# First modulation of four channel blocks: one-column products on TensorE in place of VectorE's chains of scaled additions

## The chip, the cores and the metric

The kernel runs on one core of a Trainium2 chip. A core has five engines that run their own instruction streams side by side: TensorE (PE in the profile; its weight loads are shown apart as PEld), VectorE (DVE), ScalarE (ACT), GpSimd (POOL) and SyncE (SP), which here issues the transfers. They wait for each other through semaphores. The metric is the device time of one execution in microseconds (us), the median of several runs.

## The reference, cut to what matters

The program is one layer of an encoder block on 1024 tokens with 1024 channels. Every sub-layer is wrapped in the same way:

```python
def sandwich(x, fn, g_pre, g_post, shift, scale, gate, res_w):
    h = rmsnorm(x, g_pre) * (1 + scale) + shift
    y = rmsnorm(fn(h), g_post)
    return x + res_w * gate * y

c_act = silu(c)                                   # c: one vector of 1024
mod = (c_act @ w_ada + b_ada).reshape(3, 3, 1024) # shift, scale, gate of each sub-layer
x = sandwich(x, swiglu_1, ..., mod[0, 0], mod[0, 1], mod[0, 2], 0.5)
x = sandwich(x, mixer,    ..., mod[1, 0], mod[1, 1], mod[1, 2], 1.0)
x = sandwich(x, swiglu_2, ..., mod[2, 0], mod[2, 1], mod[2, 2], 0.5)
```

The first sub-layer can't begin before its shift and scale exist: two vectors of 1024, each a product of `c_act` with a 1024 x 1024 piece of `w_ada` (4 MB apiece). `swiglu` then multiplies `h` with a gate and an up matrix of 1024 x 2816 each. All data is 32-bit float.

## The kernel before

Channels are held in 8 blocks of 128, one block on the 128 partitions; tokens in two halves of 512. A large product is made exact by splitting each operand into a high part of TensorE's reduced 32-bit format and the remainder: `hh` and `hl` for the modulated input, `wh` and `wl` for the weights. Three products (L433 to L435: hh with wh, hl with wh, hh with wl) then give one.

The change lies in `startup()`, which computes the first modulation block by block while it begins the first SwiGLU. All engines run this part in the written order (`manual_schedule` with all engines), so that an instruction that waits holds up everything behind it on its engine. For channel block j (0 to 7) the steps are:

- **Load** (L222): the 1024 x 128 pieces of `w_ada` for shift and scale, in four transfers into two tiles `rawa` (each holds 4 blocks of input channels, for both kinds).
- **Chain** (L231 to L235, VectorE): `acc` is the sum over the 8 blocks of input channels of `rawa` times the matching column of `c_act`, shift and scale side by side (128 x 256). This is done in two interleaved partial sums, two multiplications and six multiply-adds, and one addition joins them.
- **mv** (L240, TensorE): a product of `acc` with a column of ones sums over the partitions. The column (128 x 1) is what streams; `acc` is the stationary operand. There are two such products, shift and scale.
- **Set** (L245, L248, VectorE): bias and norm weight are added, which gives column j of `acol` (factor) and `scol` (shift).
- **h** (L321, L324 on ScalarE, L316 on VectorE): the transposed tokens `pt` (four transposes on TensorE, L1433) times factor plus shift, rounded into `hh`; once more unrounded into `h`; and `hl = h - hh`.
- **Parts** (`part(fb, sh, k)`): six products of 128 x 512 each, three for the gate and three for the up columns of weight block fb, with channel block k of the token half sh. Three weight blocks are begun in `startup`. Their split (`cut`, L136 on ScalarE for `wh`, L137 on GpSimd for `wl`) is queued in the same written order, so on ScalarE some splits come behind the h of a block.

In `startup` the order on TensorE is: transposes 0, mv 0, transposes 1, part(0,0,0), mv 1, transposes 2, part(0,0,1), part(1,0,0), mv 2, part(1,0,1), transposes 3, part(0,0,2), part(1,0,2), mv 3, the parts of weight block 2 with channel blocks 0 to 2, and then a loop over channel blocks 3 to 7 in which a block's chain on VectorE runs under eighteen products of the block before it. Behind the loop the second token half follows, and then sums of the halves of h on VectorE (L538, L544), which the next products need.

Of the kernel before, what the change touches and what calls it, by code (L numbers as in the profile page):

```python
# [21 lines left out]
DRAM = bass.MemoryType.DRAM  # L22
# [4 lines left out]
KB = D // P  # L27
# [13 lines left out]
SHARE = (3, 4, 4, 5, 5)  # L41
LEFT = 40.0
GATES = (2, 0, 2, 4)
NORM_ACT = ()
# [5 lines left out]
def kernel(  # L50
# [7 lines left out]
    nc = tc.nc  # L58
    x = x[0]
# [43 lines left out]
    def trbank(name):  # L103
        return ps[0].tile([P, 512], F32, tag="tr", bufs=2, name=nm(name))

# [1 line left out]
    colsA = cpool.tile([P, 104], F32, name="colsA")  # L107
# [25 lines left out]

# [1 line left out]
    def split(raw, hi, lo, eng=None):  # L135
# [19 lines left out]
    class Weights:  # L155
        """Splits the weights of a list in order, a few ahead of their use."""

# [14 lines left out]

# [1 line left out]
    c_act = cpool.tile([P, KB], F32, name="c_act")  # L174
# [62 lines left out]
    def ada_mv(acc):  # L237
# [3 lines left out]
        return pc  # L241

    def ada_set(j, pc):
        col = slice(j, j + 1)
        nc.vector.scalar_tensor_tensor(  # L245
            acol[0][:, col], pc[:, 1:2], colsA[:, 16 + j : 17 + j], colsA[:, 80 + j : 81 + j], op0=ALU.add, op1=ALU.mult
        )
        nc.vector.tensor_tensor(scol[0][:, col], pc[:, 0:1], colsA[:, 8 + j : 9 + j], op=ALU.add)  # L248
# [50 lines left out]

# [1 line left out]
    def rstd_of(src, eps):  # L301
# [36 lines left out]
    class Epilogue:  # L338
        """Residual update and next normalisation, in stages that lag the arithmetic by a token block each."""

# [50 lines left out]
        def finish(self, head, wait=HEAD_WAIT):  # L391
            """The last blocks, under the products of the next phase that need the first half only."""
            for i, _ in enumerate(head):
                if i >= wait or (self.ready and self.ready[0][0] == 0):
                    self.drain(1)
                if i == 0:
                    self.update(SB - 3)
                    self.update(SB - 2)
                    self.norm(SB - 3)
                if i == 2:  # L400
                    self.update(SB - 1)
                    self.norm(SB - 2)
                if i == 5:
                    self.norm(SB - 1)
            self.drain(KB)

        def push_last(self, sb, y, pd):
            """The last block: in halves, to end soon after the last product."""
            self.fetch(sb)
            xr = self.xr[sb]  # L410
            g = gtile[self.sub]
            sq = [small("sq"), small("sq")]
            halves = [slice(0, 512), slice(512, 1024)]
            for h, sl in enumerate(halves):
                junk = tmp[0].tile([P, D], BF16, tag="junk", bufs=2, name=nm("junk"))
                nc.vector.tensor_tensor(y[:, sl], y[:, sl], pd[h], op=ALU.add)
                nc.scalar.activation(junk[:, sl], y[:, sl], AF.Square, scale=D ** -0.5, accum_out=sq[h])
                if h == 0:
                    nc.vector.tensor_tensor(y[:, sl], y[:, sl], g[:, sl], op=ALU.mult)
            self.update(sb - 1)  # L420
            r = small("rstd")
            nc.vector.scalar_tensor_tensor(r, sq[0], self.eps, sq[1], op0=ALU.add, op1=ALU.add)
            nc.gpsimd.tensor_tensor(r, r, nhalf, op=ALU.pow)
            nc.vector.tensor_tensor(y[:, halves[1]], y[:, halves[1]], g[:, halves[1]], op=ALU.mult)
            for sl in halves:
                nc.vector.scalar_tensor_tensor(xr[:, sl], y[:, sl], r, xr[:, sl], op0=ALU.mult, op1=ALU.add)
                nc.sync.dma_start(self.xout[sb * P : (sb + 1) * P, sl], xr[:, sl])

# [1 line left out]
    def mm3(dst, w, kk, xhk, xlk, sh, first, last):  # L430
# [12 lines left out]

# [1 line left out]
    # The first column blocks of gate and up are plain products, while the halves of h are being summed. The others  # L445
    # take seven products of half blocks for eight (Strassen): with the gate [a b] and up [c e] rows of a block over
    # the halves of the channels, and h = [[w x] [y z]] over the halves of channels and tokens,
    #   1: (a+e)(w+z)  2: (c+e)w  3: a(x-z)  4: e(y-w)  5: (a+b)z  6: (c-a)(w+x)  7: (b-e)(y+z)
    #   gate = [1+4-5+7, 3+5], up = [2+4, 1-2+3+6]
    ORDER = (5, 1, 4, 6, 2, 3, 7)  # L450
    LAST_ORDER = (1, 6, 5, 4, 3, 2, 7)

    def ffn(sub, w_gu, w_down, hh, hl, xin, xout):
# [62 lines left out]

        # sums of the halves of h
        hs, dif = {}, {}
# [59 lines left out]

        # sums of the quarters of a weight block
        mixed = {}  # L580
# [81 lines left out]
        def up_phase(started):  # L662
            """All of act = silu(gate) * up, into DRAM."""
            for fb in range(started, direct):
# [5 lines left out]
            for fb in range(started, direct):  # L670
# [3 lines left out]
                finish(fb, 0)  # L674
            # what the first of the other blocks needs, in the order of its products
            def first_needs():
# [37 lines left out]

        # down projection, a few blocks of its contraction at a time
        chunks, fb0 = [], 0
# [4 lines left out]
        parts = {}  # L721

        def down_w(ci, n):
            """The n-th operand of a chunk: activations and weights of its blocks in turn."""
            if ci >= len(chunks) or n >= 2 * len(chunks[ci]):
                return
            fb, kind = chunks[ci][n // 2], n % 2
            raw = wpool.tile([P, 1024], F32, tag="raw", bufs=3, name=nm("rawd"))
            nc.sync.dma_start(raw, (act_d, w_down)[kind][fb * P : (fb + 1) * P, :])
            if kind == 0 and 0 < ci < len(chunks) - 1:  # L730
                hi, lo = (hpool.tile([P, 1024], F32R, tag="h", bufs=16, name=nm("ah")) for _ in range(2))
            elif kind == 1 and ci % 2 == 1:
                hi, lo = (wpool.tile([P, 1024], F32R, tag=t, bufs=4, name=nm("dh")) for t in ("wh", "wl"))
            else:
                hi, lo = t4("dh", F32R), t4("dl", F32R)
            split(raw, hi, lo, nc.gpsimd if kind else nc.vector)
            parts[ci, n] = hi, lo

        def down_phase(make, ahead):
# [4 lines left out]
            for sbs in (range(half), range(half, SB)):  # L744
                steps += [(ci, sb) for ci in (end - 1, end) for sb in sbs]
            # (updates, normalisations, transposed blocks of the first half) with each of the last steps
            last_steps = {
# [63 lines left out]

# [1 line left out]
    C_Q, C_K, C_V, C_XR, C_YR, C_GA, C_GR = 0, 512, 1024, 1536, 2560, 3584, 4608  # L813
# [197 lines left out]
    def att_phase(hh, hl, wts0, tg_dram, n_ga):  # L1011
        att_h, att_l = [], []
        with (
# [42 lines left out]

            # Projections as generators: one tensor-engine pass per step, cost in passes of 512.
            def pproj(w, sh):
# [74 lines left out]
            def vslice(p, h, kb):  # L1133
                # [token, block-in-tile 2, pair 2, (h0 hi, h0 lo, h1 lo, h1 hi) x 64]
                off = ((kb % 2) * 2 + p % 2) * 256 + h * P
                return vts[p // 2][kb // 2][:, off : off + P]
# [262 lines left out]

# [1 line left out]
    def startup(f1, hh, hl):  # L1401
# [40 lines left out]
        def chain(j, half):  # L1442
            ada_sum(raws[j], acc4[:, j % 2], ((0, 4, 1, 5), (2, 6, 3, 7))[half])

        def chain_seq(j, half):
            ada_sum(raws[j], acc4[:, j % 2], range(4 * half, 4 * half + 4))

        def mv(j):
            ada_set(j, ada_mv(acc4[:, j % 2]))

# [8 lines left out]
        trans(0, 0)  # L1459
        chain_seq(0, 0)  # L1460
        chain_seq(0, 1)
        f1.cut(0, 0)
        mv(0)
        trans(0, 1)
        h = h_act(0, 0)
        chain_seq(1, 0)
        h_lo(0, 0, h)
        chain_seq(1, 1)
        f1.cut(0, 1)
# [8 lines left out]
        f1.cut(1, 1)  # L1478
        chain(2, 0)
        chain(2, 1)  # L1480
        f1.part(1, 0, 0)
# [6 lines left out]
        f1.cut(2, 0)  # L1488
        chain(3, 0)
        chain(3, 1)  # L1490
        f1.cut(2, 1)
# [57 lines left out]

    # ==== program =========================================================  # L1550
    relrep = dpool.tile([HEADS, P * 767], F32, name="relrep")
# [83 lines left out]
```

## Time and profile before

| What | Value |
|---|---|
| Time, median of 3 runs | 2282.09 us (2281.98 to 2283.41) |
| Span of the profiled execution | 2280.4 us |
| TensorE busy in the span | 2212.2 us (97%) |
| VectorE, ScalarE, GpSimd busy | 1277.7, 925.0, 638.2 us |
| Mean granted TensorE clock | 0.991 of full speed |
| Transferred | 250.31 MB, mean 110 GB/s |

The profiled execution's own time is not listed apart from its span; the span runs from the first to the last instruction, and the median of the other runs is 1.7 us above it, which is what lies around it. TensorE is busy for 97% of the whole span, but that is a mean: in the first of forty slices (57 us each) it is 5 to 6 tenths busy, and in all the others 9 or more tenths. The first 50 us are the only stretch of that length in which TensorE waits for a large part.

### The profile page before, as it was taken

Reading aid. Unit: us, or ns where it says so; the run is one execution under the profiler, and the core shown is the slowest. Engines: PE = TensorE matmul, PEld = TensorE weight load, DVE = VectorE, ACT = ScalarE, POOL = GpSimd, SP = SyncE. Lnnn points to the kernel's source line nnn. Section 1 sums busy time; section 2 is a strip of 40 time slices with the busy share of each in tenths; the row PEclk is TensorE's granted clock in tenths of the full one; section 3 lists DMA queues with packets and bytes.
Section 4 is the critical chain, followed back from the end, with each engine's and each line's share of the span. In section 5 each row is a group of like instructions: output and inputs, shape, how many; then the busy total and the mean of one; then the engine's idle time right before and its main releaser. Section 6 shows DMA issues by size and latency. Waiting matters only on the chain.

```text
span 2280.4 us, 26502 instructions
## 1 busy us (share of the span) xinstructions
PE 2212.2 (97%) x10227; PEld 1837.4 (81%) x10227; DVE 1277.7 (56%) x1830; ACT 925.0 (41%) x1473; POOL 638.2 (28%) x449
## 2 busy tenths in 40 slices
PE   5989999999999999999999999999989999999998
PEld 3867888888788788888898988887878888888886
DVE  6675565545755677643336666546864444433444
ACT  3533333342223587821147777336433333342121
POOL 3433333322225311000021120006443333322324
PEclk9999999999999999999999999999999999999999
DMA  9322333345663211245312011554322222233223
GB/s 297 101 65 75 111 111 102 111 146 177 195 211 120 77 50 40 66 148 166 113 51 65 25 59 53 165 176 169 113 81 83 84 82 83 84 121 110 93 93 120
DMA packets 217749, 250.31 MB, mean 110 GB/s; under 512 B 10864, under 2 KB 172824, under 8 KB 217624
## 3 DMA queue, kind: packets, MB, share of 16 engines
q1 hardware_dynamic: 217512, 248.60, 34.7%
q8 instruction: 80, 1.31, 0.2%
q14 instruction: 45, 0.37, 0.0%
q10 hardware_dynamic: 112, 0.03, 0.0%
HBM read 203.51 MB, written 48.23 MB: 110 GB/s over the span
## 4 chain that ended last, share of the span: by engine, by line
PE 80%; DVE 8%; ACT 4%; issue 3%; DMA 2%; POOL 2%; SPq 1%; POOLq 0%; DVEq 0%; ACTq 0%
PE pd L766 19%; PE pj L433 6%; PE pj L434 6%; PE pj L435 6%; PE pj L1064 5%; PE psB L603 3%; PE psB L604 3%; PE psB L605 3%; PE psC L603 3%; PE psC L604 3%; PE psC L605 3%; PE psA L603 3%; PE psA L604 3%; PE psA L605 3%; PE pv L1111 1%
## 5 line engine op out<-in xcount | busy, mean ns | idle before, releaser
L766 PE MATMUL pd<-dh,ah 128*128 128x512 f32 x1440 | 346.9, 392 | 0.0
L766 PEld LDWEIGHTS pd<-dh,ah 128*128 128x128 f32 x1440 | 271.8, 189 | 57.0 <-POOL dh L137 0.5
L434 PE MATMUL pj<-hl,wh 128*128 128x512 f32 x576 | 226.9, 394 | 5.5 <-DVE hl L316 5.5
L779 DVE TENSOR_TENSOR yacc<-yacc,pd 128x512 f32<-128x512 f32 x190 | 121.9, 683 | 193.3 <-PE pd L766 193.2
L435 PE MATMUL pj<-hh,wl 128*128 128x512 f32 x576 | 227.1, 394 | 2.6 <-DVE wl L137 1.9
L433 PE MATMUL pj<-hh,wh 128*128 128x512 f32 x576 | 229.3, 398 | 0.0
L592 POOL TENSOR_TENSOR wsum<-raw,sr 128x512 f32<-128x512 f32 x70 | 101.0, 1443 | 318.4 <-DVE wm L596 313.8
L596 DVE TENSOR_TENSOR wm<-wsum,wm 128x512 fp32r<-128x512 f32 x185 | 146.8, 804 | 61.9 <-ACT wm L595 59.2
L595 ACT CAST wm<-wsum 128x512 fp32r<-128x512 f32 x185 | 112.5, 620 | 111.3 <-PE psB L605 83.9
L137 POOL TENSOR_TENSOR wl<-raw,wh 128x1024 fp32r<-128x1024 f32 x25 | 61.2, 2454 | 292.0 <-ACT wh L136 246.7
L136 ACT CAST wh<-raw 128x1024 fp32r<-128x1024 f32 (+1 forms) x86 | 86.8, 1011 | 129.2 <-PE pj L434 53.2
L434 PEld LDWEIGHTS pj<-hl,wh 128*128 128x128 f32 x576 | 109.4, 190 | 29.3 <-DVE hl L316 7.4
L435 PEld LDWEIGHTS pj<-hh,wl 128*128 128x128 f32 x576 | 109.3, 190 | 26.9 <-DVE wl L137 3.2
L603 PE MATMUL psB<-hh,wm 128*128 128x512 f32 x296 | 117.2, 396 | 14.1 <-DVE mixes L619 14.1
L433 PEld LDWEIGHTS pj<-hh,wh 128*128 128x128 f32 x576 | 109.5, 190 | 22.1 <-ACT hh L321 0.3
L137 DVE TENSOR_TENSOR wl<-raw,wh 128x1024 fp32r<-128x1024 f32 (+1 forms) x61 | 73.8, 1211 | 84.7 <-ACT wh L136 84.7
L604 PE MATMUL psB<-hl,wm 128*128 128x512 f32 x296 | 116.8, 395 | 0.0
L605 PE MATMUL psB<-hh,wm 128*128 128x512 f32 x296 | 116.8, 394 | 0.0
L603 PE MATMUL psC<-hh,wm 128*128 128x512 f32 x296 | 115.6, 391 | 0.5 <-ACT wm L595 0.5
L605 PE MATMUL psA<-hs,wm 128*128 128x512 f32 x296 | 115.3, 389 | 0.4 <-DVE wm L596 0.4
L605 PE MATMUL psC<-hh,wm 128*128 128x512 f32 x296 | 115.3, 390 | 0.0
L603 PE MATMUL psA<-hs,wm 128*128 128x512 f32 x296 | 115.3, 389 | 0.0
(296 smaller groups left out, 5218.0 us busy)
## 6 DMA issues: line engine op xcount, KB each, us to landing
rawa<-in_w_ada_dram SPq DMA_DIRECT2D x56, 512.0 KB, 3.7
raw<-in_ffn_w_gu_dram SPq DMA_DIRECT2D x49, 512.0 KB, 4.0
rawd<-act SPq DMA_DIRECT2D x44, 512.0 KB, 4.3
rawd<-in_ffn_w_down_dram SPq DMA_DIRECT2D x44, 512.0 KB, 4.1
raw<-in_w_in_dram SPq DMA_DIRECT2D x44, 512.0 KB, 3.8
sr<-in_ffn_w_gu_dram SPq DMA_DIRECT2D x39, 512.0 KB, 5.7
act<-act SPq DMA_DIRECT2D x37, 512.0 KB, 4.2
rawa<-in_w_ada_dram SPq DMA_DIRECT2D x32, 256.0 KB, 5.6
```

The costliest lines, as they stand in the source:

```text
L137: (eng or nc.vector).tensor_tensor(lo, raw, hi.bitcast(F32), op=ALU.subtract)
L433: nc.tensor.matmul(dst, wh[:, kk, :], xhk[:, sl], start=first, stop=False)
L434: nc.tensor.matmul(dst, wh[:, kk, :], xlk[:, sl], start=False, stop=False)
L435: nc.tensor.matmul(dst, wl[:, kk, :], xhk[:, sl], start=False, stop=last)
L595: nc.scalar.copy(t[:, 0], src)
L596: nc.vector.tensor_tensor(t[:, 1], src, t[:, 0].bitcast(F32), op=ALU.subtract)
L603: nc.tensor.matmul(dst, t[:, 0, kk, :], xh, start=first and kk == 0, stop=False, skip_group_check=True)
L604: nc.tensor.matmul(dst, t[:, 0, kk, :], xl, start=False, stop=False, skip_group_check=True)
L605: nc.tensor.matmul(dst, t[:, 1, kk, :], xh, start=False, stop=last and kk == 3, skip_group_check=True)
L766: nc.tensor.matmul(pd[h], a_[:, tk], w_[:, h * 512 : (h + 1) * 512], start=(i == 0 and j == 0), stop=(i == n - 1 and j == 2),)
L779: nc.vector.tensor_tensor(yacc[sb][:, sl], yacc[sb][:, sl], pd[h], op=ALU.add)
L1064: nc.tensor.matmul(d, a[:, k, :], b[k][:, sl], start=k == 0 and i == 0, stop=k == KB - 1 and i == 2)
```

## The change

For channel blocks 0 to 3 (`ON_PE = 4`) the chain on VectorE is left out. In its place `ada_direct` issues sixteen products on TensorE per block: for shift and for scale, eight products with the loaded `rawa` piece itself as stationary operand and one column of `c_act` as what streams, summed in the same column of PSUM. They stand at the place where the two products with the column of ones stood. Blocks 4 to 7 keep the chain. Nothing else moves in the written order; the lines of `startup` are shifted by the new function, and comments are dropped.

```diff
+ON_PE = 4
...
+    def ada_direct(raws):
+        pc = trbank("pcj")
+        for kind in range(2):
+            for k in range(KB):
+                nc.tensor.matmul(
+                    pc[:, kind : kind + 1], raws[k // 4][:, k % 4, kind, :], c_act[:, k : k + 1],
+                    start=k == 0, stop=k == KB - 1,
+                )
+        return pc
...
         def chain(j, half):
-            ada_sum(raws[j], acc4[:, j % 2], ((0, 4, 1, 5), (2, 6, 3, 7))[half])
-
-        def chain_seq(j, half):
-            ada_sum(raws[j], acc4[:, j % 2], range(4 * half, 4 * half + 4))
+            if j >= ON_PE:
+                ada_sum(raws[j], acc4[:, j % 2], ((0, 4, 1, 5), (2, 6, 3, 7))[half])
 
         def mv(j):
-            ada_set(j, ada_mv(acc4[:, j % 2]))
+            ada_set(j, ada_direct(raws[j]) if j < ON_PE else ada_mv(acc4[:, j % 2]))
...
         trans(0, 0)
-        chain_seq(0, 0)
-        chain_seq(0, 1)
         f1.cut(0, 0)
         mv(0)
         trans(0, 1)
         h = h_act(0, 0)
-        chain_seq(1, 0)
         h_lo(0, 0, h)
-        chain_seq(1, 1)
         f1.cut(0, 1)
         f1.part(0, 0, 0)
         mv(1)
...
-        chain(2, 0)
-        chain(2, 1)
         f1.part(1, 0, 0)
         mv(2)
...
-        chain(3, 0)
-        chain(3, 1)
         f1.cut(2, 1)
         f1.part(0, 0, 2)
         f1.part(1, 0, 2)
         mv(3)
```

On TensorE, before, from the last transposes of channel block 0 to the first product of the second column of block 0's part (`pcj` takes the modulation's two columns, `pj` the SwiGLU's sums):

```order
L1433 MATMUL pt_187<-ident,x_24_135 128x128
L240 MATMUL pcj_205<-ones_r,acc_17_117 128x1 x2
L1433 MATMUL pt_210<-ident,x_21_129 128x128
...
L433 MATMUL pj_232<-hh_100,wh_201 128x512
L434 MATMUL pj_232<-hl_108,wh_201 128x512
L435 MATMUL pj_232<-hh_100,wl_202 128x512
...
L435 MATMUL pj_236<-hh_100,wl_229 128x512
L240 MATMUL pcj_240<-ones_r,acc_17_117 128x1 x2
L1433 MATMUL pt_253<-ident,x_21_129 128x128
```

And the same stretch of TensorE now:

```order
L1444 MATMUL pt_187<-ident,x_24_135 128x128
L248 MATMUL pcj_196<-c_act,rawa_137 128x1 x4
L248 MATMUL pcj_196<-c_act,rawa_140 128x1 x4
L248 MATMUL pcj_196<-c_act,rawa_137 128x1 x4
L248 MATMUL pcj_196<-c_act,rawa_140 128x1 x4
L1444 MATMUL pt_215<-ident,x_21_129 128x128
...
L446 MATMUL pj_232<-hh_100,wl_225 128x512
L248 MATMUL pcj_236<-c_act,rawa_147 128x1 x4
L248 MATMUL pcj_236<-c_act,rawa_150 128x1 x4
L248 MATMUL pcj_236<-c_act,rawa_147 128x1 x4
L248 MATMUL pcj_236<-c_act,rawa_150 128x1 x4
L1444 MATMUL pt_263<-ident,x_21_129 128x128
```

Sixteen products stand where two stood, at the same place in the order: mv 1 is still behind the six products of block 0's part.

On VectorE, before, what stands between the setting of channel blocks 0 and 1:

```order
L245 SCALAR_TENSOR_TENSOR acol_81<-pcj_205,colsA 128x1 [waits PE_49]
L248 TENSOR_TENSOR scol_84<-pcj_205,colsA 128x1
L231 TENSOR_SCALAR acc_17_117<-rawa_147,c_act 128x256 [waits DMAHW6_49,DMAHW5_49]
L233 SCALAR_TENSOR_TENSOR acc_17_117<-rawa_147,c_act,acc_17_117 128x256 [waits DVE_49] x3
L316 TENSOR_TENSOR hl_108<-h_48_216,hh_100 128x512 [waits Activation_49]
L231 TENSOR_SCALAR acc_17_117<-rawa_150,c_act 128x256 [waits DMAHW7_49,DMAHW0_49]
L233 SCALAR_TENSOR_TENSOR acc_17_117<-rawa_150,c_act,acc_17_117 128x256 [waits DVE_49] x3
L235 TENSOR_TENSOR acc_17_117<-acc_17_117 128x256 [waits DVE_49]
L245 SCALAR_TENSOR_TENSOR acol_81<-pcj_240,colsA 128x1 [waits PE_49]
```

And now:

```order
L256 SCALAR_TENSOR_TENSOR acol_81<-pcj_196,colsA 128x1 [waits DVE_49,PE_49]
L259 TENSOR_TENSOR scol_84<-pcj_196,colsA 128x1
L327 TENSOR_TENSOR hl_108<-h_48_221,hh_100 128x512 [waits Activation_49]
L256 SCALAR_TENSOR_TENSOR acol_81<-pcj_236,colsA 128x1 [waits PE_49]
L259 TENSOR_TENSOR scol_84<-pcj_236,colsA 128x1
```

Nothing is left on VectorE there but the setting of the columns and the remainder `hl`. On SyncE the order of transfers is as before; the tiles that later loads reuse are now released by TensorE where VectorE released them.

## Rows read from the trace of the kernel before

**Rows 1.** Windows: time, each engine's busy us (instructions), granted clock, DMA share, GB/s.
```profile
13.40:48.40 35.00, 19.72 (x65) 13.99 (x66) 25.79 (x41) 10.18 (x12) 14.79 (x6) 0.97 1.17 294
48.40:53.30 4.90, 4.90 (x13) 3.84 (x14) 4.41 (x13) 1.45 (x2) 0.00 (x0) 0.50 1.07 381
53.30:93.30 40.00, 39.99 (x207) 33.17 (x206) 24.51 (x53) 24.72 (x36) 8.33 (x10) 1.00 0.50 141
```

**Rows 2.** Waits of TensorE, 13.4 to 48.6 us: total us, times, longest.
```profile
PE pcj L240 <- DVE acc L235: 9.0, 4, 4.9
PE pj L434 <- DVE hl L316: 5.5, 3, 4.4
```

**Rows 3.** Timeline, channel block 3: start us, us, engine, line, operation.
```profile
40.13 4.98 POOL L137 TENSOR_TENSOR sl<-sr,sh 128x1024 fp32r<-128x1024 f32 x2 [6.32 <-ACT sh L136]
40.28 6.69 DVE L233 SCALAR_TENSOR_TENSOR acc<-rawa,c_act,acc 128x256 f32<-128x256 f32 x6
```

**Rows 4.** Chain that ended last: start us, time to the next piece, what.
```profile
49.20 0.43 PE pj L434
...
55.73 0.23 PE pj L434
```

**Rows 5.** Timeline, TensorE: the last first transpose, and the four mv.
```profile
13.42 0.47 PE L1433 MATMUL pt<-ident,x 128*128 128x128 f32 x1 [1.44 <-ACT x L1424]
...
15.61 1.01 PE L240 MATMUL pcj<-ones_r,acc 128*128 128x1 f32 x4 [1.72 <-DVE acc L235]
...
27.48 0.98 PE L240 MATMUL pcj<-ones_r,acc 128*128 128x1 f32 x4 [1.91 <-DVE acc L235]
...
36.67 0.58 PE L240 MATMUL pcj<-ones_r,acc 128*128 128x1 f32 x4 [0.50 <-DVE acc L235]
...
47.58 0.98 PE L240 MATMUL pcj<-ones_r,acc 128*128 128x1 f32 x4 [4.89 <-DVE acc L235]
```

**Rows 6.** Timeline, TensorE, two later groups of eight one-column products.
```profile
379.39 1.84 PE L200 MATMUL pc<-ones_r,acc 128*128 128x1 f32 x16
...
666.57 2.54 PE L200 MATMUL pc<-ones_r,acc 128*128 128x1 f32 x16 [0.88 <-DVE acc L187]
```

**Rows 7.** Windows around the later groups of one-column products, and one without.
```profile
664.30:667.70 3.40, 2.52 (x17) 1.95 (x16) 3.13 (x4) 0.47 (x1) 0.00 (x0) 1.00 0.89 311
667.70:671.10 3.40, 3.40 (x13) 3.01 (x13) 1.58 (x3) 1.99 (x3) 2.37 (x1) 0.51 0.53 160
...
148.90:152.30 3.40, 1.56 (x7) 0.94 (x6) 3.40 (x4) 1.41 (x3) 1.84 (x2) 1.00 0.53 155
...
626.80:630.20 3.40, 3.33 (x23) 3.07 (x24) 1.38 (x4) 1.05 (x1) 0.00 (x0) 1.00 0.85 277
```

**Rows 8.** Timeline, from block 1's mv to its first product with hl.
```profile
28.89 0.78 ACT L321 ACTIVATE hh<-pt,scol,acol 128x512 fp32r<-128x512 f32 x1 [5.77 <-DVE scol L248]
29.56 0.77 ACT L324 ACTIVATE h<-pt,scol,acol 128x512 f32<-128x512 f32 x1
...
30.23 1.04 ACT L136 CAST wh<-sr 128x1024 fp32r<-128x1024 f32 x1
30.36 0.69 DVE L316 TENSOR_TENSOR hl<-h,hh 128x512 fp32r<-128x512 f32 x1 [1.57 <-ACT h L324]
...
31.11 0.79 PE L434 MATMUL pj<-hl,wh 128*128 128x512 f32 x1 [0.60 <-DVE hl L316]
...
31.34 2.46 POOL L137 TENSOR_TENSOR wl<-sr,wh 128x1024 fp32r<-128x1024 f32 x1 [5.79 <-ACT wh L136]
```

**Rows 9.** Timeline, SyncE and ScalarE: loads of later tokens, and their first use.
```profile
46.28 2.20 SPq L1411 DMA_DIRECT2D x<-in_x_dram  x4
...
63.98 1.05 ACT L304 ACTIVATE junk<-x 128x1024 bf16<-128x1024 f32 x1
```

**Rows 10.** Chain that ended last, behind the first token products.
```profile
95.49 1.87 DVE hsum L538
97.36 4.67 DMA act<-a
```

## The prediction

> **What bounds the kernel now.** I read the windows of the start first. From 13.4 us, when the first transposes end, to 48.4 us TensorE is busy for 19.7 of 35.0 us; in the next 4.9 us it never stops, though at half clock; and in the 40 us behind them it is busy for 39.99 [rows 1]. So the start is the place of the change, it has about 15.3 us of idle TensorE in it, and what ends earlier or later at 48.4 us is passed on, one for one, by a stretch without gaps. The list of waits says what TensorE idles for: 9.0 us in four waits for VectorE's chain, and 5.5 us for `hl`, which on VectorE sits between pieces of such chains [rows 2]. The timeline shows why a chain is dear: while GpSimd runs the two splits of weight block 2, VectorE's six multiply-adds take 6.69 us and end only after them [rows 3]. The reader is to see that the bound is a loop over channel blocks: modulation, then `h` and `hl`, then the parts, then the next modulation behind those parts.
>
> The clock column has to be read with care: it prints 0.97 for 13.4 to 48.4 us, but the records of the clock begin only at about 36 us. [...]
>
> **What one modulation on TensorE costs.** Two one-column products are four recorded passes [rows 5], eight are sixteen [rows 6]; sixteen products are 32. At the higher clock twelve more passes cost 1.84 - 0.58 = 1.26 us, 0.105 us each [rows 5, 6]. At the lower clock I take twice that, 0.21 us. So the 32 passes of a block take 0.58 + 28 x 0.105 = 3.5 us, or 0.98 + 28 x 0.21 = 6.9 us, where 0.6 or 1.0 us stood. The four blocks add between 4 x 2.9 = 11.7 and 4 x 5.9 = 23.5 us to TensorE, against 15.3 us of idle time of which part can't be filled. The stationary operand is a 128x128 piece of 32-bit floats in both cases, so I price the new pass by the old one.
>
> [...]
>
> **Which clock they get.** A later group of sixteen passes is the nearest row. In 664.3 to 667.7 us TensorE was busy for 2.52 us, for the last part with such passes, and the clock fell to the lower level at the end of that stretch, in the middle of the group, which took 2.54 us instead of 1.84 [rows 6, 7]. In 148.9 to 152.3 us it was busy for only 1.56 us, with 128x512 products, and the clock held; with a full stretch of products and one group (626.8 to 630.2 us) it held too [rows 7]. I read this as: one-column products keep an engine busy but do not hold the clock as wide ones do, and will not raise it. So mv 0 and mv 1, which meet a slow engine, run slow; mv 2 and mv 3 start at whatever the products before them have earned, and may lose it.
>
> [...]
>
> **The sum, step by step** (PE times; before in brackets).
> - mv 0 begins behind the last transpose, 13.9 us, and ends at 13.9 + 6.9 = 20.8 (16.6) [rows 5].
> - From the end of an mv to the first product with `hl`: in block 1, 28.46 to 31.11, 2.65 us, through `hh`, `h` on ScalarE and `hl` on VectorE [rows 5, 8]. VectorE has nothing else to do now. So block 0's: 20.8 + 2.65 = 23.5 (23.07).
> - ScalarE casts the up half of weight block 0 behind `h`, as it cast another weight at 30.23, 1.77 us after the end of mv 1; GpSimd starts 1.1 us after that cast began and takes 2.46 us [rows 8]. So its `wl` is there at 20.8 + 1.77 + 1.1 + 2.46 = 26.1 us, the last product of the part ends at 26.6, and mv 1 runs from there to 33.5 (28.46).
> - hl 1: 36.15 (31.11). Then ten products to the last of part(1,0,0), whose `wl` is there at 33.5 + 5.33 = 38.8: 10 x 0.43 = 4.3 us, to 40.5 with the clock rising near the end, as it had risen before mv 2 after five microseconds of unbroken products [rows 5]. Before, mv 2 began here at 36.67.
> - mv 2: 3.5 us if it keeps the clock, 6.9 if slow; I take 4.8, falling on the way as in [rows 6]. End 45.3 (37.25).
> - Part(1,0,1) and the transposes fill the wait for hl 2: 6 x 0.43 + 4 x 0.21 = 3.4, 48.7. Twelve products: 5.2 us slow, 2.8 fast; I take 3.5, slow at first: 52.2. The splits of weight block 2 (4.98 us on GpSimd, [rows 3]) begin behind h 2, at 45.3 + 2.9 = 48.2, and end at 53.2, under mv 3.
> - mv 3: 3.5 us, as the clock has just risen: 55.7 (48.56). The stall of its chain (4.9 us, [rows 2]) is gone, and it was not enough.
> - Then the unbroken stretch. Before, its first 4.9 us ran at the lower clock [rows 1], which lost half of them, 2.45 us. After, mv 3 may or may not cost the clock: I take 1.2 us lost.
>
> Together 55.7 - 48.56 = +7.1, less 2.45 - 1.2 = 1.25: +5.9 us. The freed VectorE buys nothing further, since `hl` needs TensorE's result first. The tiles of the later tokens are now released by mv 2 and mv 3, so their transfers go out near 46 and 56 us instead of 46 to 48; their first use was 16 us behind and moves too [rows 9]: nothing. Chains 4 to 7 stand under the unbroken stretch as before: nothing.
>
> Made against the profiled span: 2280.4 + 5.9 = 2286.3; the median lies 1.7 us above the span, so 2282.1 + 5.9 = 2288.0 us. All unknown terms at their slow end (mv 2 and mv 3 at 6.9, all parts between at 0.43, the stretch behind losing 2.45) give 47.4 + 3.4 + 5.2 + 6.9 = 62.9, +14.3 us. All at their fast end are the first rival.
>
> **Rivals.**
> - One-column products do raise and hold the clock. mv 0 ends at about 20.3, `wl` of block 0 is ready at 25.6, mv 1 runs 26.0 to 29.5, hl 1 at 32.2, mv 2 35.2 to 38.7 (behind its `wl`), hl 2 41.4, twelve products to 44.1, mv 3 to 47.6; and the stretch behind is fast at once: 47.6 - 48.56 - 2.45 = -3.4, 2278.7 us. For it: the group at 379.39 us kept its clock, 1.84 us for its sixteen passes [rows 6]. [...] Against it: the fall at 667.7 us [rows 6, 7]. Chance 0.14. It is the case on the other side, and it decides once mv 1 runs in about 3.6 us.
> - The clock stays low throughout mv 2 to mv 3: +9 to +14 us, 2291 to 2296. For it: five microseconds of unbroken wide products stood before the rise in the kernel before, and no run of them between the mv's is longer. Against: part(0,0,1) and part(1,0,0) stand together. Chance 0.16.
> - The delay is made, but partly given back: behind the token halves the chain that ends last goes through VectorE's sums of h and waits 4.67 us for a store [rows 10]. If that store goes by the traffic of the loads and not by TensorE, it absorbs up to 4.7 us: 2283.3 to 2285. For it: the store shares its queue with weight loads. Against: the queue is as late as TensorE then. Chance 0.12.
>
> **How the numbers follow.** Forecast 2288.0 us with 0.58; its own range is 2285 to 2291 (mv 2 and the products behind it vary by 3 us either way). 0.2% is 4.6 us, about what a measurement of this kernel can tell from no change. Slower by more: 0.44 of the forecast's 0.58, and 0.16 of the low clock: 0.60. Faster by more needs over 4.6 us gained, beyond the first rival's sum: 0.03. Within: the rest, 0.37. The range runs from 2279.5, into the first rival, to 2293.5, into the second.
>
> **What would show it.** In the profile after, mv 0 as 32 passes of some 6.9 us in all, and mv 1 likewise, would bear the price out; mv 2 with two pitches would bear the clock out. No wait of TensorE for a chain before mv 4; `hl` still waited for, 2.6 us behind each mv; mv 3 ending near 55.7 us. The forecast is wrong if mv 1 ends before 31 us, if a one-column pass at the lower clock costs well under 0.21 us, or if the time at which the sums of h begin (95.5 us before, [rows 10]) has not moved by the same 6 us.

## The result, and the profile after

The changed kernel takes 2290.55 us (median of 5 executions, 2288.15 to 2292.98), the kernel before 2282.4 us (5 executions beside them): a ratio of 1.0034, 95% interval [1.0023, 1.0045]. It is slower, by 8 us in the medians; forecast were 5.9 us, a time of 2288.0 and a range to 2293.5. The profiled execution took 2292.98 us, the slowest of the five; its span is 2291.2 us, 10.8 above the one before.

The start in windows (columns as in [rows 1]):

```profile
13.40:48.40 35.00, 32.40 (x135) 28.08 (x136) 2.93 (x9) 10.09 (x13) 10.28 (x5) 0.95 1.15 284
...
53.30:93.30 40.00, 40.00 (x204) 33.40 (x204) 25.03 (x62) 24.12 (x36) 7.07 (x10) 0.96 0.55 159
```

TensorE is now busy for 32.4 of the 35.0 us in which it was busy for 19.7, and VectorE for 2.9 where it was for 25.8 [rows 1]. The waits of TensorE in the start are almost gone (13.4 to 62 us, columns as in [rows 2]):

```profile
PE pj L445 <- DVE hl L327: 1.2, 2, 0.6
...
PE pj L446 <- POOL wl L138: 0.6, 1, 0.6
```

So 14.5 us of waits [rows 2] have become 1.8, 12.7 less, and the kernel is slower. What fills the gap is seen in TensorE's timeline, which answers to [rows 5]:

```profile
13.46 0.47 PE L1444 MATMUL pt<-ident,x 128*128 128x128 f32 x1 [1.43 <-ACT x L1435]
13.73 6.83 PE L248 MATMUL pcj<-c_act,rawa 128*128 128x1 f32 x32
...
26.45 6.82 PE L248 MATMUL pcj<-c_act,rawa 128*128 128x1 f32 x32
...
40.77 3.87 PE L248 MATMUL pcj<-c_act,rawa 128*128 128x1 f32 x32
...
50.74 3.63 PE L248 MATMUL pcj<-c_act,rawa 128*128 128x1 f32 x32
```

The four mv take 6.83, 6.82, 3.87 and 3.63 us, 17.6 us more than the four before [rows 5]. The end of mv 3, which lets the stretch without gaps begin, is at 54.37 us; it was at 48.56. So 17.6 us of work more and 12.7 us of waits less account for 4.9 of these 5.8 us. The granted clock in windows cut where it changed:

```profile
41.30:44.70 3.40, 3.40 (x31) 3.40 (x32) 0.02 (x1) 0.00 (x0) 0.00 (x0) 1.00 1.09 256
44.70:48.10 3.40, 3.40 (x11) 2.69 (x11) 0.96 (x3) 3.04 (x4) 0.58 (x1) 0.50 0.98 253
48.20:54.90 6.70, 6.70 (x47) 6.12 (x46) 0.49 (x4) 0.30 (x2) 4.03 (x2) 1.00 0.90 267
55.00:58.30 3.30, 3.30 (x9) 2.54 (x8) 3.04 (x8) 1.23 (x2) 0.00 (x0) 0.50 0.92 330
```

mv 2 begins half a microsecond before the clock rises (at 41.28 us), hence its 3.87 us. TensorE has no idle moment from 36.5 us to the end of these windows, and still the clock falls twice, each time behind a group of one-column products (mv 2 and mv 3); it is at 0.50 from 44.7 to 48.1 us and from 54.9 to 58.35 us, and back at 1.00 behind 128x512 products. VectorE's sums of h, the first work behind the stretch, start 5.1 us later than in [rows 10]:

```profile
100.62 1.91 DVE L549 TENSOR_TENSOR hsum<-top,bot 128x512 f32<-128x512 f32 x1
```

The start thus accounts for 5.1 us. Matching VectorE's instructions of the two traces one by one shows where the other 5.7 us of this execution come in: the shift against the kernel before is 5.5 us at 500 us, 9.4 at 700, 9.3 at 1500 and 10.8 at the end.

### The profile page after: what moved, and what is told of

Read it like the earlier page. It is cut to its first block, busy times and chain, and to the rows that moved or that the text cites. A ratio compares the mean times of both kernels' runs of the same rounds, so it can differ in the third digit from the quotient of the medians.

```text
span 2291.2 us, 26683 instructions
## 1 busy us (share of the span) xinstructions
PE 2231.2 (97%) x10339; PEld 1856.5 (81%) x10339; DVE 1250.6 (55%) x1794; ACT 925.0 (40%) x1473; POOL 636.5 (28%) x449
## 4 chain that ended last, share of the span: by engine, by line
PE 80%; DVE 8%; ACT 4%; issue 3%; DMA 3%; POOL 2%; SPq 0%; POOLq 0%; DVEq 0%; ACTq 0%
PE pd L777 17%; PE pj L445 6%; PE pj L446 6%; PE pj L444 6%; PE pj L1075 5%; PE psB L614 3%; PE psB L615 3%; PE psB L616 3%; PE psC L614 3%; PE psC L615 3%; PE psA L614 3%; PE psC L616 3%; PE psA L615 3%; PE psA L616 3%; PE pv L1122 1%
## 5 line engine op out<-in xcount | busy, mean ns | idle before, releaser
L616 PE MATMUL psA<-hs,wm 128*128 128x512 f32 x296 | 115.3, 390 | 0.4 <-DVE wm L607 0.4
L615 PE MATMUL psC<-hl,wm 128*128 128x512 f32 x296 | 115.3, 390 | 0.0
```

Source lines behind the costliest of these rows:

```text
L615: nc.tensor.matmul(dst, t[:, 0, kk, :], xl, start=False, stop=False, skip_group_check=True)
L616: nc.tensor.matmul(dst, t[:, 1, kk, :], xh, start=False, stop=last and kk == 3, skip_group_check=True)
```

## The experiments

Each is the changed kernel or the one before with the edit shown; all were run beside the kernel before, whose median on those chips was 2282.3 to 2283.0 us.

**The same kernel again, twice.** No edit.

> The changed kernel once more, for a second profile. In the first one the start-up is 5.1 us late where VectorE's sums of h begin (95.5 us before), and the end 10.8 us late; most of the rest comes between 540 and 640 us, where the background's one-column products stand. Theory A (the later part is the granted clock, which falls or holds at such groups as chance has it): sums of h again 4 to 8 us late, but the later shift differs, by steps of about 1.7 or 3.4 us. Theory B (the late start sets queues and loads of the down projection differently, the same in every execution): again 5 to 6 us more between 540 and 640 us.

Measured: one execution, 2290.74 us. The four mv last as in the first profile (mv 2 3.71 us), and the clock falls behind mv 2 and mv 3 as there; the sums of h start 4.9 us late (100.40). Between 500 and 700 us another 3.7 us are lost, which spoke for theory B. Hence a third profile:

> The changed kernel for a third profile and more times. Two profiles were 4 and 3 us later again between 540 and 690 us, on top of the 5 us of the start-up. Theory A (chance of the granted clock and of loads there): this profile loses 0 to 2 us in that stretch, as six other kernels did, and the median over these executions lies 5 to 7 us above before. Theory B (the same in every execution of this kernel): again 3 to 4 us there, and a median 8 us above before.

Measured: 2289.31 us (median of 6, 2286.43 to 2294.54; ratio 1.003 [1.0018, 1.0042]). The start is again 4.9 us late, by another way: the clock falls once, inside mv 2, stays low from 43.87 to 50.70 us, and does not fall behind mv 3.

```profile
40.70 3.94 PE L248 MATMUL pcj<-c_act,rawa 128*128 128x1 f32 x32
...
52.04 3.63 PE L248 MATMUL pcj<-c_act,rawa 128*128 128x1 f32 x32
```

The stretch from 500 to 700 us adds 0.8 us, and at the end the shift is 4.2 us. So in three profiles the start costs 5.1, 4.9 and 4.9 us, and all that follows adds 5.7, 3.6 and -0.7. The start's share is the change. The later share differs between executions of one program, so theory B, the same loss in every execution, falls. What decides it is only partly seen. Two windows each from the first and the third profile of the changed kernel, at the first of the background's two later groups, where the clock fell in both:

```profile
631.00:635.00 4.00, 2.02 (x13) 1.45 (x11) 3.88 (x3) 0.00 (x0) 2.26 (x1) 1.00 0.48 155
635.20:642.00 6.80, 6.80 (x23) 5.74 (x23) 0.50 (x2) 1.05 (x1) 0.00 (x0) 0.50 0.56 198
```
```profile
630.00:634.30 4.30, 2.78 (x21) 2.32 (x20) 3.31 (x4) 0.11 (x1) 0.86 (x1) 1.00 0.60 205
634.40:637.80 3.40, 3.40 (x10) 2.63 (x9) 0.00 (x0) 0.83 (x1) 0.00 (x0) 0.50 0.69 251
```

It stayed low for 6.8 us in the one and 3.4 in the other, which is 1.7 us of time. The other traces narrow this down. Of the seven profiles of kernels with blocks 0 to 3 on TensorE (these three and four of the runs below), three add 3.2 to 3.9 us between 500 and 700 us, and in each of these the clock is low for 10.2 us there; four add 0.5 to 0.9, with 6.8 us of low clock, as in the kernel before. The six profiles of the other edits add -0.1 to 0.6. So the lower clock makes about 1.7 us of the large losses. What makes the rest stays open; VectorE's waits for the background's pieces of `w_ada` are longer in the three profiles above (12.6, 10.8 and 10.2 us, 8.1 before), the one with the small loss included. The medians of the changed kernel's two timed sets lie 8.2 and 6.3 us above before, more than the start's 5, so a mean extra of 1 to 3 us is likely. That the large losses came with four blocks on TensorE alone speaks for the change, but three profiles of seven do not prove it.

**Does a one-column product raise the clock?** Two kernels answer it. In the first, block 0's sixteen products are issued three times:

```diff
-        for kind in range(2):
-            for k in range(KB):
+        for _ in range(times):        # 3 for channel block 0
+            for kind in range(2):
+                for k in range(KB):
```

> The sixteen products of channel block 0 are issued three times over (the last sum counts). Theory A (one-column products do not raise the clock): 96 passes at 0.213 us, one unbroken stretch of 20.5 us at the lower level, 13.7 us later at mv 1. Rival (sustained activity of any kind raises it, mv 0 was just too short): the spacing falls to 0.11 us after at most 7 us, and the stretch takes 12 to 14 us.

```profile
13.69 20.48 PE L249 MATMUL pcj<-c_act,rawa 128*128 128x1 f32 x96
```

Measured (one execution, 2298.86 us): 96 passes in 20.48 us, 0.213 each from the first to the last. Twenty microseconds of unbroken passes did not raise the clock. In the second, 32 wide products stand ahead of the sixteen:

```diff
         pc = trbank("pcj")
+        if wide is not None:          # channel block 0: a split weight block, 512 columns of it
+            for _ in range(32):
+                nc.tensor.matmul(pc, ones_r, wide, start=True, stop=True)
```

> Ahead of channel block 0's sixteen products stand 32 products of 128x512 into the same bank (a column of ones times weights, overwritten afterwards), 13.7 us at the lower clock if it never rose. Theory A: the clock rises within them after 3 to 7 us, so they take 8 to 10 us; the one-column products behind start at 0.11 us a pass and fall back to 0.21 on the way or soon after. Rival (it is time, not width): the same rise, but the one-column products of blocks 0 and 1 then hold the higher level throughout.

```profile
16.24 9.05 PE L248 MATMUL pcj<-wh,ones_r 128*128 128x512 f32 x32 [2.25 <-ACT wh L137]
25.13 3.62 PE L251 MATMUL pcj<-c_act,rawa 128*128 128x1 f32 x32
...
34.64 6.82 PE L251 MATMUL pcj<-c_act,rawa 128*128 128x1 f32 x32
```

Measured (one execution, 2298.14 us): the wide products raise the clock at 19.2 us, 3 us after their start, and end in 9.05 us. mv 0 then takes 3.62 us in place of 6.83. The clock falls at 29.4 us, 0.7 us behind its end, and mv 1 is back at 6.82. Theory A's times came in both kernels: the time spent in unbroken work does not decide alone. That the width does is not shown, since the two kinds of product differ in type too: the wide ones are in TensorE's reduced 32-bit format, the one-column ones in full 32 bits. Over all traces sixteen such groups of 32 passes met the higher clock. It fell inside or within 1 us behind thirteen of them, and held behind three.

**Which block costs what.** The choice of blocks becomes a tuple, and the left-out chains stand where they stood before:

```diff
-ON_PE = 4
+ON_PE = (3,)          # then (0,), (1,) and (0, 1)
...
-            if j >= ON_PE:
+            if j not in ON_PE:
```

> Only channel block 3 takes its modulation from TensorE, blocks 0 to 2 keep VectorE's chain. Theory A (a block gains when the chain's stall is longer than its 32 passes at the clock they meet): TensorE has been at the higher clock since about 36 us, mv 3 starts when the twelve products end (42.5 us) and takes 3.5 us, so it ends at 46.0 in place of 48.6, and the stretch behind loses about 1 us to the lower clock in place of 2.45: 3 to 4 us faster than before, about 2279. Rival (the splits of weight block 2 on GpSimd, which end at 45.1 us, or hl 3 hold TensorE instead): the parts of weight block 2 wait and the gain is under 1 us, 2281.5 to 2283.

Measured: 2279.95 us (11 executions), ratio 0.9987 [0.9978, 0.9996]: faster, by 2.3 us in the medians where 3 to 4 were expected. Its mv 3, and the sums of h:

```profile
42.73 3.63 PE L248 MATMUL pcj<-c_act,rawa 128*128 128x1 f32 x32
```
```profile
91.08 1.91 DVE L549 TENSOR_TENSOR hsum<-top,bot 128x512 f32<-128x512 f32 x1
```

mv 3 ends at 46.36 us, 2.2 earlier, and in this execution the clock did not fall behind it, so the 2.45 us of [rows 1] are saved whole: the start is 4.4 us early. The expectation had let 1 us of that go. The end of mv 3 came near the expected 46.0; the median gain is smaller than the profiled execution's, whose mean granted clock, 0.994, is the highest of the eleven (0.991 to 0.993 in the others). So the 4.4 us are in part a good execution's.

> Only channel block 0 on TensorE, blocks 1 to 3 keep the chain. Theory A (a later mv costs only what nothing else was late by): mv 0 ends at 20.6 us, 4 us later, but hl 0 was at 23.1 in any case, held by the chain of block 1; that chain is late by little, mv 1 ends near 29.2 instead of 28.5, and the whole is 0.5 to 1.5 us slower, 2283 to 2284. Rival (each block passes on what its products cost, 4 us of the 5 come from here): 2286.

Measured: 2284.23 us (10 executions), 1.0005 [0.9996, 1.0014]; the start 1.3 us late. mv 0 is 4 us late, as expected, but mv 1 ends at 30.85 us, 1.6 later than I had it. The chain of block 1 stands behind the setting of block 0 on VectorE and begins at 20.97 us where it began at 18.54, 2.4 us later, and it wins nothing back. Its first half now meets no split on GpSimd, but the second meets two; before, each half met one, and the six multiply-adds took 7.0 us (3.48 and 3.57), as they do here.

```profile
21.35 1.52 DVE L234 SCALAR_TENSOR_TENSOR acc<-rawa,c_act,acc 128x256 f32<-128x256 f32 x3
...
23.77 5.49 DVE L234 SCALAR_TENSOR_TENSOR acc<-rawa,c_act,acc 128x256 f32<-128x256 f32 x3
```

> Only channel block 1 on TensorE. Theory A: hl 0 is no longer behind the chain, so part(0,0,0) ends near 22.6 us and mv 1 runs from there to 29.4, 1 us later than before: 2283 to 2284. Rival (each block passes on its cost): mv 1 ends near 33.3 us as in the changed kernel, 4 to 5 us slower, 2287.

Measured: 2284.05 us (10 executions), 1.0006 [0.9997, 1.0015]; the start 0.9 us late. mv 1 begins at 22.86 and ends at 29.68 us:

```profile
22.86 6.82 PE L248 MATMUL pcj<-c_act,rawa 128*128 128x1 f32 x32
```

> Channel blocks 0 and 1 on TensorE, 2 and 3 keep the chain. Theory A: the two stand one behind the other with the handoff of block 0 and its part between them, mv 1 ends at 33.3 us as in the changed kernel, and from there on nothing gives it back: mv 3 ends near 53, 4 to 5 us slower than before, 2286 to 2288, more than the sum of the two alone. Rival (costs add): the sum of what the two alone cost.

Measured: 2287.21 us (10 executions), 1.0017 [1.0008, 1.0027]; the start 4.7 us late (100.18). Alone the two cost 1.3 and 0.9 us of the start, together 4.7: costs don't add. (Ahead of the change these traces already differ by up to half a microsecond: the last of the first transposes starts at 13.42 us before and at 13.63, 13.67 and 13.94 in these three. The times agree: alone neither differs from before beyond its interval, together they do.) Either of them is nearly hidden as long as the other block's step, on VectorE, would have been late too; with both on TensorE the 6.8 us stand one behind the other. Blocks 0 and 1 make up nearly all of the changed kernel's 5 us. Block 3 on TensorE gains 4.4 us of the start in its trace, 2.3 us in the median, when blocks 0 to 2 keep the chain; with blocks 0 to 2 on TensorE the same step starts at 50.74 us, behind two mv of 6.8 us and one of 3.87 us that itself lost the clock. Block 2 alone was not run.

**Why block 3's chain was long.** The kernel before, with the two splits of weight block 2 on VectorE:

```diff
-            split(raw, hi, lo, nc.gpsimd if fb < direct and sub == 0 or fb == 1 else nc.vector)
+            split(raw, hi, lo, nc.gpsimd if fb < direct and sub == 0 and not spare or fb == 1 else nc.vector)
```

> The kernel before, with the two splits of weight block 2 on VectorE in place of GpSimd, in the same written order. Theory A (chain 3 is long because GpSimd runs these splits at the same time): its six multiply-adds take 2.5 us instead of 6.7, each split 1.2 us, mv 3 ends near 46 instead of 48.6 us: 2 to 3 us faster, 2279.5 to 2280.5. Rival (the multiply-adds are slow by themselves or by the loads): they still take over 6 us, and the splits come on top, 2 us slower.

```profile
41.99 2.46 DVE L233 SCALAR_TENSOR_TENSOR acc<-rawa,c_act,acc 128x256 f32<-128x256 f32 x6
```

Measured: 2280.06 us (10 executions), 0.9985 [0.9975, 0.9994]. The six multiply-adds take 2.46 us where they took 6.69 [rows 3], and mv 3 ends at 45.6 us. GpSimd's splits made the chain long; the arithmetic did not. In the trace of the kernel before, two of the six take 2.62 and 2.56 us, each begun just behind the start of a split of 2.5 us and ended 0.28 us behind its end, and the other four 0.47 each. The traces show these times, not what holds VectorE up.

**Filling the waits.** The changed kernel with mv 1, 2 and 3 ahead of the parts they stood behind:

```diff
         f1.cut(0, 1)
-        f1.part(0, 0, 0)
         mv(1)
+        f1.part(0, 0, 0)
...
-        f1.part(0, 0, 1)
...
-        f1.part(1, 0, 0)
         mv(2)
+        f1.part(0, 0, 1)
+        f1.part(1, 0, 0)
...
+        mv(3)
         f1.part(0, 0, 2)
         f1.part(1, 0, 2)
-        mv(3)
```

> The changed kernel, with mv 1, mv 2 and mv 3 moved ahead of the parts they stood behind, so that they fill TensorE's waits for hl. Theory A (TensorE is full: 32.4 of 35.0 us busy between 13.4 and 48.4 us, so what counts is the clock of the passes): the 2.6 us of waits go, but mv 2 meets a slow engine and takes 6.8 in place of 3.9 us; the stretch without gaps begins 0 to 2 us earlier than in the changed kernel, 2288 to 2290. Rival (the loop is bound by the handoff through ScalarE and VectorE, which the move hides): 5 us and more off the changed kernel, near 2284.

```profile
22.47 6.99 PE L248 MATMUL pcj<-c_act,rawa 128*128 128x1 f32 x32 [0.42 <-ACT h L335]
...
32.87 6.83 PE L248 MATMUL pcj<-c_act,rawa 128*128 128x1 f32 x32
```

Measured: 2286.97 us (10 executions), 1.0019 [1.0009, 1.0029], 1 us under the expected stretch. The sums of h start 1.7 us earlier than in the changed kernel (98.94). mv 2 takes 6.83 us as expected: what was won in waits is partly paid for with the lower clock. TensorE was busy for 34.1 of the 35.0 us from 13.4 us on, and the gain is far from 5 us: with the handoff hidden, what is left is the passes and the clock they meet.

**A version that beats the kernel before and the changed one.** Block 3 alone on TensorE, and the splits of weight blocks 0 to 2 on VectorE:

```diff
-            split(raw, hi, lo, nc.gpsimd if fb < direct and sub == 0 or fb == 1 else nc.vector)
+            split(raw, hi, lo, nc.gpsimd if fb == 3 and sub == 0 or fb == 1 and sub == 2 else nc.vector)
```

> Only channel block 3 on TensorE, and the splits of the first weight blocks 0 to 2 on VectorE in place of GpSimd. Theory A (chains 1 and 2 lose 2 to 2.5 us each to GpSimd's splits of weight blocks 0 and 1): mv 1 ends near 26.5 us instead of 28.6, mv 2 near 35 instead of 37.4, mv 3 near 44: 1.5 to 2.5 us faster than with block 3 alone, 2277.5 to 2278.5. Rival (the loads of the later tokens or of w_ada are by then the bound): mv 3 is early, but the loop over blocks 3 to 7 waits and the sums of h begin where they do with block 3 alone: 2280.

```profile
25.67 0.85 PE L241 MATMUL pcj<-ones_r,acc 128*128 128x1 f32 x4
...
34.08 0.58 PE L241 MATMUL pcj<-ones_r,acc 128*128 128x1 f32 x4
...
39.93 3.62 PE L248 MATMUL pcj<-c_act,rawa 128*128 128x1 f32 x32
```

Measured: 2277.01 us (10 executions), 0.9978 [0.9969, 0.9987], half a microsecond under the expected range. mv 1, 2 and 3 end at 26.5, 34.7 and 43.6 us, each earlier than with block 3 alone (mv 3 by 2.8). The sums of h start at 89.80 us, 1.3 earlier than there: the clock fell behind mv 3 this time, from 43.95 to 47.36 us, and took the rest.

**The later falls, made wider.** The changed kernel, with the one-column products of the background's groups (the kind in [rows 6]) 64 columns wide:

```diff
-                pc[:, k : k + 1], acc[:, k * P : (k + 1) * P], ones[:, 0:1], start=True, stop=True
+                pc[:, k * 64 : (k + 1) * 64], acc[:, k * P : (k + 1) * P], ones[:, 0:64], start=True, stop=True
```

> The changed kernel, with the background's later groups of one-column products made 64 columns wide (64 equal columns, of which one is used): 16 passes stream 1024 columns where they streamed 16. Theory A (the clock falls near 635 and 676 us because one-column passes and the waits ahead of them leave TensorE with few columns): at least one of the two falls is gone, 1.7 to 3.4 us less between 540 and 690 us than the changed kernel. Rival (the falls come from the waits for VectorE's sums alone): both falls stay, no change beyond 0.5 us.

```profile
632.85 2.00 PE L201 MATMUL pc<-ones_r,acc 128*128 128x64 f32 x16 [1.73 <-DVE acc L188]
...
675.16 2.88 PE L201 MATMUL pc<-ones_r,acc 128*128 128x64 f32 x16 [1.89 <-DVE acc L188]
```

Measured: 2287.48 us (11 executions), 1.0021 [1.0012, 1.003]. Both falls stay (635.1 to 638.5 and 676.1 to 682.9 us). The median is 1.8 us under that of the changed kernel beside it, but the two intervals overlap. Theory A missed: 64 columns don't hold the clock there, with a wait of 1.7 to 1.9 us ahead of the group. The rival's sign came, both falls stay; that the waits alone cause them is not shown by it, since the group is still there.

## Why the prediction was right

- **Price of a pass.** 32 passes were put at 6.9 us at the lower clock and 3.5 at the higher. Measured 6.83 and 6.82 (mv 0, 1), and 3.63 where the clock held for the whole group (mv 3).
- **Which clock.** One-column products were expected not to raise the clock and to risk it. Three times the group leaves it low for 20.48 us, and behind wide products the same group runs fast once (3.62 us) and then loses it, 0.7 us behind its end. The first rival needed mv 1 in 3.6 us; it took 6.82, and the rival fell. That mv 0 and mv 1 would meet the lower clock is to be read from the products around them in the trace before: 128x512 products stood 0.43 us apart where the granted clock was 0.50 and 0.23 where it was 1.00 [rows 1, 4], and ahead of the clock's records the unbroken ones, 23.66 to 24.94 and 31.70 to 35.54 us, started 0.43 apart as well. The 0.43 us a product in the sum is this spacing. The rows that the reading was drawn from [rows 7] were weaker than it: the view that they are from has two more windows without a one-column product, behind which the clock fell as well (at 1449.39 and 1589.34 us), with TensorE busy for 1.47 of 3.30 and 1.70 of 3.40 us, so falls came behind such half-idle stretches too.

```profile
1446.00:1449.30 3.30, 1.47 (x9) 1.12 (x8) 1.96 (x4) 1.56 (x4) 0.00 (x0) 1.00 0.45 143
1585.90:1589.30 3.40, 1.70 (x7) 0.77 (x5) 3.40 (x3) 2.75 (x5) 2.22 (x2) 1.00 0.03 8
```

- **The steps.** The end of mv 0 was put at 20.8 us and came at 20.56; mv 1 33.5 and 33.27; mv 2 from 40.5 to 45.3, and it was 40.77 to 44.64; the twelve products behind it to 52.2, and it was 50.74, since the clock had risen at 48.1; mv 3 55.7, and it was 54.37. The loss to the lower clock in the stretch behind was taken as 1.2 us and is about 1.7 (half of 54.9 to 58.35 us). Sum 5.9, measured at the sums of h 5.1, 4.9 and 4.9. The near agreement is in part luck: mv 3 ended 5.8 us later and not 7.1, mostly since mv 2 took 3.87 us where 4.8 were put, and the clock behind it gave back 0.7 us and not 1.25.
- **What was not in the sum.** The later shift, 5.7 us in the first profile, 3.6 and -0.7 in the others. I had let everything behind 93 us move one for one. The size of the forecast (5.9 of 8.2 us) is short by this, not by a step of the start, and that the time still came out near the forecast owes something to a start put 0.8 to 1 us too dear.
- **Two passes for a product.** Sixteen products left 32 records, two for each, in 6.83 us (mv 0): 0.213 us a record, where 0.21 was put.
- **The other rivals.** A clock low through mv 2 and mv 3 did not occur: in all three profiles mv 3 ran at the higher level throughout (3.63 us each) and mv 2 for most of its time (it rose 0.5 and 0.1 us into mv 2 in the first two, and 0.2 us ahead of it in the third). The give-back behind the token halves did not occur: the shift was 5.1 us at 95 us and 5.5 at 500 us.

## What to carry to other kernels

Count what a new TensorE job does to TensorE's own path, not only what wait it removes: here it removed 12.7 us of waits and put 17.6 us of passes in their place, 6.8 us for each of the first two blocks, which met the lower clock. A step of a serial loop is worth moving where its present stall is longer than its price at the clock it will meet, which held for one of the three blocks run alone (block 3). And when an engine's instruction is many times its usual length, look first at which other engine ran just then: moving two splits gave about the same gain in the median (2.7 us) as moving the work of block 3 (2.3).

## What the runs showed of the hardware that was not expected

- TensorE busy without a gap still lost its clock. After nearly nothing but one-column products (the window 41.30 to 44.70 us, busy throughout, granted 1.00) it fell to 0.50, and over all traces it fell inside or within 1 us behind thirteen of sixteen such groups; 20.5 us of nothing but such passes never raised it (96 in 20.48 us, 0.213 each); 32 products of 128x512 raised it 3 us after they began (at 16.24 and 19.2 us).
- VectorE's multiply-adds of 128x256, about 0.41 us from one to the next (2.46 for six), took 6.69 for six, and 5.49 for three, where GpSimd was splitting weights at the same time.
- Executions of one unchanged program differ by up to 6 us in what they lose between 500 us and the end, with the sums of h in place to 0.3 us.
